# Second mixer of a two-layer encoder trunk: the half swaps before the scans are issued from ScalarE's queue instead of SyncE's

## The chip, the cores and the metric

The kernel runs on one core of a Trainium2 chip. The metric is the device time of one execution in microseconds (us); the median over the runs shown is compared. The profile is one further execution, with its own time. TensorE is PE in the profile (its weight load is PEld), VectorE is DVE, ScalarE is ACT, GpSimd is POOL, SyncE is SP. A trailing q (SPq, ACTq) marks the engine's instruction queue, which among other things issues DMAs.

## The reference, cut to what matters

The trunk has two layers on 512 positions of width 1024. Each layer is a mixer, a cross-attention into 256 memory tokens, and a gated convolutional FFN. The change lies in the mixer of the second layer, in its bidirectional S5 state-space half:

```
bu_re = einsum('gph,bsgh->bsgp', bb_re, u);  bu_im = einsum('gph,bsgh->bsgp', bb_im, u)
s = associative_scan(s_t = a * s_(t-1) + bu_t)          # complex, once forward, once backward
y = einsum('ghp,bsgp->bsgh', c_re, s_re) - einsum('ghp,bsgp->bsgh', c_im, s_im)
o_c = gelu(y_f + y_b + d_skip * u) * sigmoid(...)
```

The other half of the mixer is a depthwise convolution of width 31 with a gate and a layer norm. Both halves are projected out together.

## The kernel before

The 512 channels of the S5 part are four blocks (i = 0 to 3), each with two directions (d = 0 forward, 1 backward). Real parts of the states lie on partitions 0 to 63 of a tile and imaginary parts on 64 to 127. A complex rotation therefore needs the tile once as it is and once with its halves swapped. A swap is two DMAs, from one half of the partitions to the other half of a second tile, 128 KB each.

The work of a block runs through stages with one-letter names. The list `CD` at the top of the kernel gives their order by hand, such as `c0 C0 q0 k1 a1 v1 V1 q0 q0 s0 b1 l1 L1`. The stages that matter here:

- `u`, `v`, `g`: projections of 24 matmuls (lines 206 to 208) of 128x512, with a weight load `wr` of 512 KB from SP (line 147), a high part `wh` cut on ACT (line 201) and a low part `wl` on DVE or POOL (line 202).
- `l`, `L`: SP loads the input matrices `bm` (line 1358) and the rotation tables `cst` (line 1363) of a block.
- `c`, `C`: `c_(i, 0)` and `c_(i, 1)`, the function that the diff touches. 8 matmuls of 64 columns (line 1374) give a tile, ACT copies it to T1 (line 1377), two DMAs write T1s (1378, 1379), DVE multiplies by the tables and adds (1380 to 1382), scans (1384 or 1386) and rotates back (1387, 1388).
- `s`: the second swap, T1s to X2s, from SP (1394, 1395). `x`: the sum with it (1402), on DVE or POOL.
- `m`: SP loads three matrices `cm` (1408). `y`: the output matmuls with them (1416, 1418).
- `q`: two taps of the convolution on DVE (1463). `w`, `Z`: tables `ct` from SP (1476) and the convolution as matmuls (1489). `a`, `b`, `A`, `B`: transposes (1336, 1345) with ACT copies (1337, 1353). `f`: gelu of the block (1431, 1433). `k`: one step of the next stage's keys and values, with its own weight loads.

A planner with its own costs orders the instructions of each engine when the program is built. For most stages `pinned` adds that the first instruction of a stage on PE and the first on SP stay behind those traced before them; a `q` is held so on DVE. ACT isn't held. Every engine and every queue takes its instructions strictly in the planned order, so an SP DMA that waits holds up all later DMAs of SP. A weight load also waits until one of three `wr` buffers is free; `cm` has three buffers and `ct` two.

ACT issues DMAs at only one other place, line 581 in the first mixer.

Of the kernel before, what the change touches and what calls it, by code (L numbers as in the profile page):

```python
# [90 lines left out]
def trunk(ctx, tc, xT, memT, pos, vec, amask, cmask, bmask,  # L91
          w_z, w_ab, w_abv, w_oab, w_xq, w_xk, w_xv, w_xo, w_up, w_dn, wg2,
          w_cd, w_glu, w_ocd, s5v, s5b, s5bs, s5c, s5cs, ctab, out, upto=99):
    nc = tc.nc
# [8 lines left out]
    def nm(p):  # L103
        n_[0] += 1
        return f"{p}_{n_[0]}"
# [32 lines left out]
    def tp_ps():  # L138
        return PS.tile([128, 512], F32, tag="tp", bufs=2, name=nm("tp"))
# [1118 lines left out]
    def mixer_cd(norm, nnext, kv):  # L1258
# [3 lines left out]
        def b2(tag, bufs):  # L1262
            return T.tile([128, S], F32, tag=tag, bufs=bufs, name=nm(tag))
# [101 lines left out]
        def c_(i, d):  # L1365
            BM, cst = tab[i, d], rot[i, d]
            ct, st, rt = cst[:, 0], cst[:, 1], P.tile([128, S], F32, tag="nsq", bufs=2, name=nm("rt"))
            A.activation(g3(rt), rho[:, 32 * d + 8 * i:32 * d + 8 * i + 8].unsqueeze(2).to_broadcast([128, 8, 64]),
                         AF.Copy)
            V.memset(g3(rt)[:, :, 63 * d:63 * d + 1], 0.0)  # L1370
            fl = (lambda v: g3(v)) if d == 0 else (lambda v: g3(v)[:, :, ::-1])
            tp = tp_ps()
            for g in range(8):
                PE.matmul(tp[:, 64 * g:64 * g + 64], BM[:, 128 * g:128 * g + 128], Rg[i][:, 64 * g:64 * g + 64],  # L1374
                          start=True, stop=True)
            t1, t1s = b2("T1", 3), b2("T1s", 2)
            A.activation(t1, tp, AF.Copy)
            nc.sync.dma_start(t1s[0:64], t1[64:128])
            nc.sync.dma_start(t1s[64:128], t1[0:64])
            V.tensor_tensor(g3(t1), g3(t1), fl(ct), ALU.mult)  # L1380
            V.tensor_tensor(g3(t1s), g3(t1s), fl(st), ALU.mult)
            V.tensor_tensor(t1, t1, t1s, ALU.add)
            if d == 0:
                V.tensor_tensor_scan(t1s, rt, t1, 0.0, op0=ALU.mult, op1=ALU.add)
            else:
                V.tensor_tensor_scan(t1s[:, ::-1], rt[:, ::-1], t1[:, ::-1], 0.0, op0=ALU.mult, op1=ALU.add)
            V.tensor_tensor(g3(t1), g3(t1s), fl(ct), ALU.mult)
            V.tensor_tensor(g3(t1s), g3(t1s), fl(st), ALU.mult)
            X[i, d] = t1, t1s
# [139 lines left out]
        def k_(i):  # L1529
            for _ in range(min(i, len(ksteps))):  # L1530
                if ksteps[0] == kv.norm:
# [5 lines left out]
        stage = {"u": (PS_, u_), "a": (PS_, a_), "b": (PS_, b_), "x": ((), x_), "y": (PS_, y_),  # L1537
                 "l": (PS_, l_), "L": (PS_, r_), "m": (PS_, m_), "s": (PS_, s_),
                 "c": (PS_, lambda i: c_(i, 0)), "C": (PS_, lambda i: c_(i, 1)),
                 "f": (PS_, f_), "v": (PS_, lambda i: half0(4 + i)), "V": (PS_, v_),  # L1540
                 "g": (PS_, lambda i: half0(8 + i)), "G": (PS_, g_),
# [192 lines left out]
```

## Time and profile before

| What | Value |
|---|---|
| median of 3 runs | 1631.38 us (1629.17 to 1634.59) |
| profiled execution, its own time | 1632.09 us |
| span of the profiled execution | 1630.3 us |
| busy: PE, DVE, ACT, POOL | 96%, 66%, 43%, 23% of the span |
| mean granted TensorE clock | 0.982 of full speed |
| second mixer's S5 blocks | about 875 to 1050 us in the span |

The span runs from the first to the last instruction; 1.8 us of the execution's own time lie outside it. Busy shares are averages over stages with different limits. In the rows below a bracket is the idle time of the engine just before an instruction and what ended it.

### The profile page before, as it was taken

What the parts mean: (1) busy time and instruction counts of PE and PEld (TensorE: products, weight loads), DVE (VectorE), ACT (ScalarE), POOL (GpSimd) and SP (SyncE); (2) the same over time, 40 slices, a digit from 0 to 9 for tenths busy, and PEclk for the clock granted to TensorE, in tenths of its full rate; (3) what the DMA queues carried; (4) which work ended last, traced back from release to release, by engine and by line L of the source; (5) the groups of instructions that cost most, each with busy time, mean ns of one, the idle gap of its engine ahead of it and who ended that gap; (6) DMA issues with size and microseconds to landing.
All of it is one profiled execution on the core that took longest, in us unless ns stands there. A gap on an engine that the chain in (4) does not pass through costs nothing.

```text
span 1630.3 us, 20958 instructions
## 1 busy us (share of the span) xinstructions
PE 1570.0 (96%) x8036; PEld 1313.0 (81%) x8036; DVE 1079.4 (66%) x1475; ACT 707.4 (43%) x1089; POOL 368.2 (23%) x371
## 2 busy tenths in 40 slices
PE   8999999999999898989999898989999999999997
PEld 6788889888888777877887777878888888888887
DVE  7587766466578789489655997275755766636644
ACT  5464755354453334234335233364543544414423
POOL 8411000000079844445500101230000111100101
PEclk9999999999999999999999899999999999999999
DMA  5323334131222345435444574533312232323231
GB/s 176 109 78 90 120 98 134 51 117 52 78 87 91 105 128 153 145 110 163 145 157 148 181 279 128 186 127 135 108 40 78 92 102 92 102 92 103 83 112 64
DMA packets 76118, 189.11 MB, mean 116 GB/s; under 512 B 8369, under 2 KB 27441, under 8 KB 76017
## 3 DMA queue, kind: packets, MB, share of 16 engines
q1 hardware_dynamic: 75376, 186.58, 35.5%
q8 instruction: 63, 1.03, 0.3%
q0 software_dynamic: 320, 1.05, 0.2%
q14 instruction: 39, 0.31, 0.1%
q10 hardware_dynamic: 320, 0.13, 0.0%
HBM read 162.43 MB, written 19.01 MB: 111 GB/s over the span
## 4 chain that ended last, share of the span: by engine, by line
PE 69%; DVE 13%; POOL 6%; DMA 3%; issue 3%; ACT 3%; SPq 1%; ACTq 0%; DVEq 0%; POOLq 0%
PE mm L208 20%; PE mm L206 19%; PE mm L207 19%; DVE wl L202 2%; PE mm L737 2%; PE sc L1489 1%; DVE t L972 1%; DVE dv L1463 1%; DVE t L971 1%; PE tp L724 1%; PE tp L1374 1%; POOL t L1139 1%; POOL wl L202 1%; DVE tr L1138 1%; PE sc L206 1%
## 5 line engine op out<-in xcount | busy, mean ns | idle before, releaser
L201 ACT ACTIVATE wh<-wr 128x1024 fp32r<-128x1024 f32 (+1 forms) x229 | 239.1, 1044 | 419.7 <-PE mm L207 316.8
L208 PE MATMUL mm<-hg,wl 128*128 128x512 f32 x1000 | 393.7, 394 | 13.8 <-DVE wl L202 13.4
L206 PE MATMUL mm<-hg,wh 128*128 128x512 f32 x1000 | 398.3, 398 | 2.0 <-ACT wh L201 2.0
L207 PE MATMUL mm<-hg,wh 128*128 128x512 f32 x1000 | 392.8, 393 | 0.0
L202 DVE TENSOR_TENSOR wl<-wr,wh 128x1024 fp32r<-128x1024 f32 (+1 forms) x215 | 279.0, 1298 | 68.3 <-ACT wh L201 66.3
L208 PEld LDWEIGHTS mm<-hg,wl 128*128 128x128 f32 x1000 | 189.7, 190 | 57.5 <-DVE wl L202 16.2
L206 PEld LDWEIGHTS mm<-hg,wh 128*128 128x128 f32 x1000 | 190.1, 190 | 44.4 <-ACT wh L201 2.7
L207 PEld LDWEIGHTS mm<-hg,wh 128*128 128x128 f32 x1000 | 189.8, 190 | 40.0 <-issue 1.2
L208 PE MATMUL mm<-g,wl 128*128 128x512 f32 x324 | 126.7, 391 | 2.4 <-DVE wl L202 2.4
L206 PE MATMUL mm<-g,wh 128*128 128x512 f32 x324 | 126.9, 392 | 0.0
L207 PE MATMUL mm<-g,wh 128*128 128x512 f32 x324 | 126.2, 389 | 0.0
L976 POOL TENSOR_TENSOR t<-t,t 128x512 f32<-128x512 f32 x22 | 28.9, 1314 | 422.8 <-ACT t L182 422.8
L968 DVE TENSOR_TENSOR u<-mm,R 128x512 f32<-128x512 f32 x88 | 60.3, 687 | 74.2 <-PE mm L208 74.0
L970 ACT ACTIVATE t<-u,vt 128x512 f32<-128x512 f32 x88 | 70.8, 807 | 50.0 <-DVE u L968 49.8
L986 DVE TENSOR_TENSOR h<-mm,h 128x512 f32<-128x512 f32 x40 | 27.6, 691 | 87.9 <-PE mm L208 87.9
L971 DVE SCALAR_TENSOR_TENSOR t<-u,vt,t 128x511 f32<-128x511 f32 x88 | 77.3, 879 | 8.1 <-ACT t L970 8.1
L972 DVE SCALAR_TENSOR_TENSOR t<-u,vt,t 128x511 f32<-128x511 f32 x88 | 79.2, 901 | 4.1 <-DMA dct<-tr 1.5
L208 PEld LDWEIGHTS mm<-g,wl 128*128 128x128 f32 x324 | 60.8, 188 | 16.1 <-DVE wl L202 3.2
L182 ACT ACTIVATE t<-t 128x512 f32<-128x512 f32 x44 | 27.8, 632 | 103.5 <-DVE t L972 103.4
L207 PEld LDWEIGHTS mm<-g,wh 128*128 128x128 f32 x324 | 60.9, 188 | 12.4
L206 PEld LDWEIGHTS mm<-g,wh 128*128 128x128 f32 x324 | 60.9, 188 | 12.4
L202 POOL TENSOR_TENSOR wl<-wr,wh 128x1024 fp32r<-128x1024 f32 x14 | 35.0, 2503 | 140.7 <-ACT wh L201 121.5
(522 smaller groups left out, 3040.9 us busy)
## 6 DMA issues: line engine op xcount, KB each, us to landing
wr<-in_w_up SPq DMA_DIRECT2D x88, 512.0 KB
wr<-in_w_dn SPq DMA_DIRECT2D x32, 448.0 KB
wr<-in_w_ab SPq DMA_DIRECT2D x16, 512.0 KB
wr<-in_w_xv SPq DMA_DIRECT2D x16, 512.0 KB
wr<-in_w_xk SPq DMA_DIRECT2D x16, 512.0 KB
wr<-in_w_xq SPq DMA_DIRECT2D x16, 512.0 KB
wr<-in_w_xo SPq DMA_DIRECT2D x16, 512.0 KB
wr<-in_w_dn SPq DMA_DIRECT2D x16, 512.0 KB
```

What stands on the lines that cost most here:

```text
L182: tabbed(A.activation(dst, src, fn, **kw))
L201: A.activation(H[:, :n], raw[:, :n], AF.Copy)
L202: (eng or V).tensor_tensor(L[:, :n], raw[:, :n], H[:, :n].bitcast(F32), ALU.subtract)
L206: PE.matmul(ps, lH, rH, start=start, stop=False)
L207: PE.matmul(ps, lH, rL, start=False, stop=False)
L208: PE.matmul(ps, lL, rH, start=False, stop=stop)
L737: PE.matmul(onat[:, 64 * j:64 * j + 64], pt[:, 128 * jt:128 * jt + 128], va[:, jt, 64 * hd:64 * hd + 64], start=jt == 0, stop=jt == 3)
L968: V.tensor_tensor(u, ps, R, ALU.mult)
L970: A.activation(t, u, AF.Identity, scale=vc(f"cw{l}", 44 + i), bias=vc(f"cb{l}", i))
L971: V.scalar_tensor_tensor(t[:, 1:], u[:, :S - 1], vc(f"cw{l}", i), t[:, 1:], op0=ALU.mult, op1=ALU.add)
L972: V.scalar_tensor_tensor(t[:, :S - 1], u[:, 1:], vc(f"cw{l}", 88 + i), t[:, :S - 1], op0=ALU.mult, op1=ALU.add)
L976: (V if l == 0 else G).tensor_tensor(res[1], res[1], res[0], ALU.mult)
```

## The change

The two DMAs that swap the halves of T1 are issued from ScalarE's queue. There they stand on the engine that makes their source, T1. The second swap (`s`) stays on SP, as do all loads.

```
@@ c_(i, d)
             t1, t1s = b2("T1", 3), b2("T1s", 2)
             A.activation(t1, tp, AF.Copy)
-            nc.sync.dma_start(t1s[0:64], t1[64:128])
-            nc.sync.dma_start(t1s[64:128], t1[0:64])
+            nc.scalar.dma_start(t1s[0:64], t1[64:128])
+            nc.scalar.dma_start(t1s[64:128], t1[0:64])
             V.tensor_tensor(g3(t1), g3(t1), fl(ct), ALU.mult)
```

`c_` runs eight times, so 16 DMAs change queues. A stage `c` or `C` then holds no SP instruction that could be pinned.

## Rows read from the trace of the kernel before

**Rows 1.** The page: busy time and share of each engine; chain that ended last.
```profile
PE 1570.0 (96%) x8036; PEld 1313.0 (81%) x8036; DVE 1079.4 (66%) x1475; ACT 707.4 (43%) x1089; POOL 368.2 (23%) x371
...
PE 69%; DVE 13%; POOL 6%; DMA 3%; issue 3%; ACT 3%; SPq 1%; ACTq 0%; DVEq 0%; POOLq 0%
```

**Rows 2.** Windows: stretch, length, busy time by engine, granted clock, DMA share, GB/s.
```profile
940.00:960.00 20.00, 16.63 (x96) 13.34 (x96) 19.93 (x30) 5.40 (x9) 0.00 (x0) 0.93 0.65 234
960.00:980.00 20.00, 20.00 (x115) 17.42 (x114) 16.45 (x25) 10.13 (x17) 2.68 (x1) 0.90 0.89 325
```

**Rows 3.** SP's own waits, 866 to 1030 us: total, times, longest.
```profile
SPq L1378 <- ACT T L1377: 58.3, 6, 19.1
SPq L1394 <- DVE T1s L1388: 34.0, 6, 10.3
```

**Rows 4.** Chain of waits in the second mixer: start, us, what.
```profile
890.85 0.61 ACT T L1377
...
892.06 2.37 DMA T1s<-T
...
918.33 2.37 DMA T1s<-T
...
953.84 5.49 DMA cm<-dc
...
997.78 4.08 DMA T1s<-T
...
1025.34 5.75 DMA wr<-in_w_xv
```

**Rows 5.** Lines 1378, 1379 and 581: ns min/median/max of one DMA issue.
```profile
L1378 SPq DMA_DIRECT2D T1s<-T x8: 461/467/549, 891.5 to 997.3; - x8
L1379 SPq DMA_DIRECT2D T1s<-T x8: 582/588/590, 892.1 to 997.8; - x8
L581 ACTq DMA_DIRECT2D d_rt<-rt x4: 342/444/448, 68.1 to 69.4; - x4
```

**Rows 6.** SP's timeline: start, length, line, DMA, count.
```profile
908.08 0.48 SPq L147 DMA_DIRECT2D wr<-in_w_xv  x1
...
918.97 0.58 SPq L1408 DMA_DIRECT2D cm<-dmt  x1
...
937.10 0.45 SPq L147 DMA_DIRECT2D wr<-in_w_cd  x1
...
953.35 0.87 SPq L1408 DMA_DIRECT2D cm<-dc  x2
...
998.46 1.68 SPq L1476 DMA_DIRECT2D ct<-in_ctab  x2
1000.24 0.86 SPq L147 DMA_DIRECT2D wr<-in_w_xv  x2
```

**Rows 7.** ACT's timeline behind the second copy of block 0.
```profile
893.12 0.58 ACT L1337 ACTIVATE at<-tp 64x512 f32<-64x512 f32 x1
```

**Rows 8.** PE's timeline: first output matmul of block 1 (y1).
```profile
956.80 0.91 PE L1416 MATMUL sc<-cm,Rg 128*64 128x128 f32 x4 [2.10 <-DMA cm<-dmt]
```

**Rows 9.** Windows around the output matmuls of block 1, then block 2 (columns as rows 2).
```profile
956.80:966.20 9.40, 8.83 (x49) 7.88 (x50) 8.66 (x14) 2.71 (x5) 0.00 (x0) 0.64 0.80 300
996.50:1002.00 5.50, 5.50 (x50) 5.29 (x49) 2.05 (x4) 1.19 (x2) 0.00 (x0) 1.00 0.85 215
```

**Rows 10.** DVE's timeline, 920 to 1002 us.
```profile
920.78 0.69 DVE L1380 TENSOR_TENSOR T<-T,cst 128x512 f32<-128x512 f32 x1 [0.78 <-DMA T1s<-T]
...
963.61 1.23 DVE L202 TENSOR_TENSOR wl<-wr,wh 128x1024 fp32r<-128x1024 f32 x1
...
969.83 0.42 DVE L245 SCALAR_TENSOR_TENSOR macc<-tp,macc 128x256 f32<-128x256 f32 x1 [0.71 <-ACT macc L244]
...
973.45 0.69 DVE L1327 TENSOR_TENSOR uT<-mm,R 128x512 f32<-128x512 f32 x1 [0.50 <-PE mm L208]
...
1001.94 0.69 DVE L1380 TENSOR_TENSOR T<-T,cst 128x512 f32<-128x512 f32 x1 [1.39 <-DMA T1s<-T]
```

## The prediction

> **What bounds the kernel now.** I read the page first. PE is busy for 96% of the span and carries 69% of the chain that ended last, and the queues of SP and ACT carry about 1% of it together [rows 1]. A DMA issue alone is therefore worth almost nothing over the whole kernel. What counts is whether something in the second mixer stands behind an issue. The windows came next. From 940 to 960 DVE is busy for 19.93 of 20 us and PE for only 16.63, so here DVE sets the pace and PE waits. From 960 to 980 PE is full again, at a granted clock of 0.90, and the DMAs move 325 GB/s [rows 2]. Then I asked what SP waits for. For 58.3 us, in six waits of up to 19.1 us, it stands at line 1378 until ACT has written T1. That wait is what the change takes off SP. A second of its kind, 34.0 us at the swaps behind the scans, stays [rows 3]. Last I followed the chain of waits through the blocks, to see which of the things queued on SP behind the first wait end late enough to matter.
>
> **The swap itself.** The chain shows ACT's copy of block 0 starting at 890.85 and lasting 0.61 us. The DMA's own part starts at 892.06, at the start of the second issue, and takes 2.37 us to the first DVE multiply; the same 2.37 us stands at 918.33 for block 1 [rows 4]. Between them lies SP's first issue, 0.47 us in the median; the second takes 0.59 [rows 5]. The copy ends at 891.46 and the second issue starts at 892.06, so 0.60 us passes in which the first issue takes most: SP starts as good as at once, and no handshake of size is there to be saved. ACT's own DMA issues exist in this trace, at line 581: 0.44 us in the median, for a smaller transfer of another shape [rows 5]. Bounds for the two issues together are thus 0.88 us (twice that row) and 1.06 us (SP's rows). A gain of 0.2 us per swap is the most, over the three or so swaps on the chain 0.6 us. I take SP's values, as the transfer is the same one, and so a gain of 0.
>
> **What ACT pays.** Sixteen issues of about 0.53 us are 8.4 us more on ACT's queue. The cover is ACT's idle time: it is busy for 5.40 us of 20 and 10.13 of 20 in the two windows [rows 2]. Behind a swap stand the next copy of T1, the `wh` cut of a projection, and copies of transposes. The one place that is tight is block 0: right behind the copy for the backward direction ACT starts a transposes' copy of 0.58 us at 893.12, and a second such one follows in the code [rows 7]. If these two go ahead of the second swap, that swap is up to 1.2 us late and DVE with it; if the swap goes first, the copies are late and PE has 24 matmuls in front of the work that needs them. The code has the swap first, so I take 0 and keep the 1.2 us for the range.
>
> **What SP gains, and where it ends.** The loads queued behind the eight swaps leave earlier. Three groups count.
>
> *Block 1's `cm`.* After its weight load at 937.10 SP issues nothing until the swaps of block 2, and two of the three `cm` loads follow behind these at 953.35 [rows 6]. Their buffers were block 0's, whose output matmuls stand well ahead in `CD`, so I see only the wait for T1 between. The chain runs through this transfer, 5.49 us of it [rows 4]. PE waits 2.10 us for it [rows 8] and then needs 9.40 us at a granted clock of 0.64, where block 2's same work takes 5.50 us at clock 1.00 [rows 9]. So 2.10 + (9.40 - 5.50) = 6.0 us is what PE would gain if `cm` lay ready. I don't book it in full, because DVE stands behind it. The next projection needs `wl`, which DVE makes at 963.61 in an unbroken row of work [rows 10]; an earlier PE waits there. DVE itself waits for the PE and ACT work that would come earlier only 0.71 us at 969.83 and 0.50 us at 973.45 [rows 10]. DVE's order kept, 1.2 us passes on.
>
> *Block 1's own swaps.* The `cm` and weight loads that now leave at 918.97 [rows 6] are block 0's, find their buffers unused, and can leave behind the weight load at 908.08 [rows 6], about ten microseconds earlier. So they are in flight when block 1's swaps go. DVE waits for the second of these, 0.78 us [rows 10], and is nearly full afterwards, so a later landing is a loss of the same size. From below, the landing stays at 2.37 us, which is what it takes with the `cm` issue right behind it; the nearest row with a costly neighbour is the 4.08 us at 997.78, with `ct` right behind at 998.46 [rows 4, 6], 1.71 more. The upper end is a landing like that of a load on a busy queue, 5.75 us [rows 4], 3.4 more. Of the two near rows one says 0 and one 1.7; I take the middle, a loss of 0.9 us.
>
> *Block 3's swaps.* The `ct` and weight loads of 998.46 and 1000.24 move ahead of the swaps that they now follow [rows 6]. DVE waits 1.39 us for the second swap [rows 10]. If those loads are done by then, 4.08 becomes 2.37 and 1.7 us is won; if they are in full flow, 4.08 becomes 5.75 and 1.7 us is lost. They would leave when the convolution's matmuls have freed the `ct` buffers, which is shortly before the swaps and so between the two; I take 0.
>
> The row at 997.78 says that transfers of one queue already slow one another here. The Trainium skill, page "DMA: Bandwidth & Descriptors", section "Issuing engines are not separate DMA queues", speaks against the change: DMAs issued by different engines run on the same 16 DMA engines, and a second issuer saves only issue time on the sequencer. By that rule alone the sum would be 0 for the swaps and their 8.4 us on SP would fall into its waits; the row agrees in so far as a load beside a swap costs the swap time.
>
> **Sum.** 0 for the issue, 0 on ACT, 1.2 gained at block 1's outputs, 0.9 lost at its swaps, 0 at block 3: 0.3 us gained. The profiled execution took 1632.09 us (span 1630.3 and 1.8 around it), so 1631.8 by its time. It lies 0.7 above the median of the runs, 1631.38; in their terms the forecast is 1631.1. Its own range is from 1.2 + 1.7 + 0.6 = 3.5 gained to 1.2 - 3.4 - 1.7 - 1.2 = 5.1 lost with all bounds at once; 1628 to 1635 is what I give it.
>
> **Rivals.** *The gain at `cm` passes on.* The planner orders DVE and ACT anew, and with SP free it may set `wl` and the scans of block 2 earlier. Then all 6.0 us reach the end: 1625.4, or 1623.7 with block 3's 1.7 as well. For it speaks that PE has this time to give [rows 8, 9]; against it that DVE is full for 20 us [rows 2] and none of its work is removed.
>
> *The swaps collide with the released loads.* This one ends slower. On a queue of their own the swaps share the DMA engines with everything that SP no longer holds back. If each lands like the loads beside it, in 5.75 us, block 1 loses 3.4, block 2 as much (at most, since the chain doesn't run through its swaps) and block 3 1.7, together 8.5 less the 1.2 gained: 1638.7. It decides where 4.9 us are lost net, from an extra of 2.6 us per swap on (2.6 + 2.6 + 0.9 - 1.2), a landing of 5.0 us. For it speak the DMA share of 0.89 in the window from 960 and 0.80 to 0.85 beside the outputs [rows 2, 9]; against it that the swap at 918.33 landed in 2.37 us with three loads issued behind it.
>
> *Nothing moves.* The swaps behind the scans hold SP too, 34.0 us [rows 3], and the loads may be held by them, by buffers, or by the planned order, and leave when they leave now. Then it is 1631.4.
>
> **Numbers.** Forecast 0.45, nothing moves 0.17, gain passes on 0.19, collision 0.13; 0.06 is for a reordering with effects elsewhere, shared between both signs. A measurement of this kernel can tell about 0.3% from no change, 4.9 us. That gives faster 0.22, same 0.61, slower 0.17. The range runs from 1626 to 1637 and leaves out the outer parts of both rivals.
>
> **What would show it.** The T1s DMAs on ACT's queue, 0.03 us or so behind the copy, with landings between 2.4 and 4.1 us; SP's wait at line 1378 gone, its time now at 1394; `cm` of block 1 issued near 938, no wait before line 1416, and block 1's outputs in about 5.5 us at full clock; and then PE waiting for `wl` or DVE near 962. The forecast fails if DVE's order around 953 to 975 changes, if swaps land later than 5 us, or if ACT sets a `wh` cut of 1 us between T1 and its swap on the chain.

## The result, and the profile after

The change makes the kernel slower. Its median is 1642.65 us (10 runs, 1639.88 to 1654.63) beside 1634.15 us for the kernel before (10 runs, 1629.17 to 1637.11), a ratio of 1.0066 with a 95% interval of 1.0047 to 1.0085. The medians are 8.5 us apart, and 0.66% of 1634.15 is 10.8 us. The forecast was 1631.1 us with a range from 1626 to 1637. The profiled execution took 1640.68 us with a span of 1638.9; the kernel before took 1632.09 with 1630.3. So 8.6 us are to be found.

The page of the changed kernel shows next to nothing of it. Busy times stand as they stood, and the chain's shares within three points [rows 1]. ScalarE's queue, q10, has 1600 packets where it had 320.

```profile
PE 1570.4 (96%) x8036; PEld 1311.1 (80%) x8036; DVE 1077.7 (66%) x1475; ACT 707.9 (43%) x1089; POOL 367.2 (22%) x371
...
q1 hardware_dynamic: 74096, 184.48, 34.8%
q10 hardware_dynamic: 1600, 2.23, 0.6%
...
PE 72%; DVE 12%; POOL 6%; issue 3%; DMA 3%; ACT 3%; SPq 1%; ACTq 0%; DVEq 0%; POOLq 0%
```

The windows, with the columns of [rows 2], show where it happens. From 920 to 940 the DMAs are nearly idle and DVE is less busy than it was (19.18 us before); from 940 to 960 PE works 12.57 of 20 us, where it worked 16.63, and its granted clock is 0.74 in place of 0.93 [rows 2].

```profile
920.00:940.00 20.00, 20.00 (x124) 16.70 (x122) 16.89 (x23) 4.60 (x9) 2.65 (x1) 1.00 0.12 31
940.00:960.00 20.00, 12.57 (x61) 9.82 (x60) 18.60 (x25) 5.40 (x7) 1.26 (x1) 0.74 0.92 336
960.00:980.00 20.00, 20.00 (x128) 16.46 (x128) 15.63 (x28) 9.65 (x18) 0.00 (x0) 1.00 0.41 119
```

To size a loss one needs marks that every kernel has. I take the start of ACT's copy of T1 (line 1377) in the forward direction of each block. Before, it starts at 890.85, 913.78, 949.63 and 994.86 us for blocks 0 to 3; after, at 891.70, 914.41, 958.78 and 1003.76. From block 0 to block 1 nothing is lost (22.93 and 22.71). From block 1 to block 2 it is 35.85 before and 44.37 after, so **8.5 us are lost there**. From block 2 to block 3 it is 45.23 and 44.98. One stretch carries everything. ACT's timeline before:

```profile
913.78 0.60 ACT L1377 ACTIVATE T<-tp 128x512 f32<-128x512 f32 x1 [2.68 <-PE tp L1374]
...
949.63 1.16 ACT L1377 ACTIVATE T<-tp 128x512 f32<-128x512 f32 x2
```

And after:

```profile
958.78 0.60 ACT L1377 ACTIVATE T<-tp 128x512 f32<-128x512 f32 x1 [0.37 <-PE tp L1374]
```

DVE's timeline in that stretch, two lines of the kernel before and then the changed kernel:

```profile
917.50 0.69 DVE L1380 TENSOR_TENSOR T<-T,cst 128x512 f32<-128x512 f32 x1 [1.15 <-DMA T1s<-T]
...
925.45 0.67 DVE L1327 TENSOR_TENSOR uT<-mm,R 128x512 f32<-128x512 f32 x1
```

```profile
920.06 1.23 DVE L202 TENSOR_TENSOR wl<-wr,wh 128x1024 fp32r<-128x1024 f32 x1 [2.91 <-ACT wh L201]
924.33 0.69 DVE L1327 TENSOR_TENSOR uT<-mm,R 128x512 f32<-128x512 f32 x1 [3.05 <-PE mm L208]
924.94 0.74 DVE L1463 SCALAR_TENSOR_TENSOR dv<-dv,vt,dv 128x509 f32<-128x509 f32 x1
925.60 2.84 DVE L1380 TENSOR_TENSOR T<-T,cst 128x512 f32<-128x512 f32 x1
```

The order is new. Before, DVE took the first multiply of block 1 (L1380) at 917.50, then `wl`, the second multiply at 920.78 [rows 10], the scans, and block 2's projection sum (L1327) only at 925.45. After, the planner has `wl`, the sum and a tap ahead of the first multiply. DVE stands 2.91 us for `wh` and 3.05 us for block 2's matmuls, and the multiply starts at 925.60 with no bracket: it waits for its place and for no transfer. Its 2.84 us in place of 0.69 stand beside a `wl` of GpSimd's at 925.24; before, a tap at 927.92 took 2.85 beside the same `wl` at 927.88, so this is no part of the loss.

The chain that ended last says how this reaches PE (start, us, what):

```profile
910.73 7.06 PE tp L1374 x32
...
924.94 0.74 DVE dv L1463
925.68 2.75 DVE T L1380
...
932.77 1.13 DVE T1s L1384
...
939.95 1.19 DVE T1s L1388 x2
...
941.84 0.47 SPq L1394
...
943.63 4.23 DMA wr<-in_w_xv
947.90 0.04 issue
947.95 1.07 ACT wh L201
949.01 0.04 issue
949.05 0.80 PE mm L206
```

The multiplies are 8 us late, and with them the scans and the rotation back (L1388). SP issues the second swap at 941.84 where it did at 932.67. Behind it on SP stands a weight load, which lands 4.23 us after its issue, then `wh` is cut, and only then PE has work. PE's timeline gives the larger part of the price, to which the lower clock of that window adds; before, it shows no wait between 926 and 952 us:

```profile
947.76 0.80 PE L206 MATMUL mm<-hg,wh 128*128 128x512 f32 x1 [7.35 <-ACT wh L201]
```

SP's timeline shows the loads. `cm` of block 0 leaves at 909.30, ten microseconds before its 918.97 in [rows 6], `cm` of block 1 at 946.61 in place of 952.72. SP's wait for T1 of [rows 3] is gone; SP now waits at line 1394, for the first swap's landing (46.2 us) and for the scans (45.8; before, 34.0).

```profile
909.30 0.46 SPq L1408 DMA_DIRECT2D cm<-dmt  x1
...
940.57 0.47 SPq L1394 DMA_DIRECT2D X2s<-T1s  x1
...
943.63 0.45 SPq L147 DMA_DIRECT2D wr<-in_w_xv  x1
...
946.61 0.39 SPq L1408 DMA_DIRECT2D cm<-dmt  x1
```

SP's waits, in total, times and longest:

```profile
SPq L1394 <- DMA T1s<-T: 46.2, 4, 15.2
SPq L1394 <- DVE T1s L1388: 45.8, 5, 18.1
```

ACT's timeline: the swap is issued 0.03 us behind its copy (914.41 + 0.60 = 915.01), and the second issue of the backward swap runs beside the `wh` cut, at 918.98.

```profile
914.41 0.60 ACT L1377 ACTIVATE T<-tp 128x512 f32<-128x512 f32 x1 [2.53 <-PE tp L1374]
915.04 0.47 ACTq L1378 DMA_DIRECT2D T1s<-T  x1
915.55 0.61 ACTq L1379 DMA_DIRECT2D T1s<-T  x1
...
918.97 1.06 ACT L201 ACTIVATE wh<-wr 128x1024 fp32r<-128x1024 f32 x1 [0.55 <-ACT T L1377]
918.98 0.59 ACTq L1379 DMA_DIRECT2D T1s<-T  x1
```

Last, the queues of the changed kernel: packets, MB and share of the 16 engines' time, from 917 to 919 us and then from 919 to 921.

```profile
q1 hardware_dynamic: 219, 0.79, 100.9%
q10 hardware_dynamic: 1, 0.00, 0.3%
...
q1 hardware_dynamic: 129, 0.46, 69.5%
q10 hardware_dynamic: 125, 0.22, 36.1%
```

The forward swap was issued by 916.2. In the first of these windows SP's queue fills the engines with its released loads and ScalarE's moves one packet.

Two causes are thus in sight. **Order:** VectorE's planned order in block 1 puts block 2's sum ahead of the multiplies. **Landing:** the released loads hold up the swaps, and the order only fills the time until they land. They are the theory and its rival in what follows.

### The profile page after: what moved, and what is told of

Its sections match the earlier page's. It is cut to its first block, busy times and chain, and to the rows that moved or that the text cites. A ratio compares the mean times of both kernels' runs of the same rounds, so it can differ in the third digit from the quotient of the medians.

```text
span 1638.9 us, 20960 instructions
## 1 busy us (share of the span) xinstructions
PE 1570.4 (96%) x8036; PEld 1311.1 (80%) x8036; DVE 1077.7 (66%) x1475; ACT 707.9 (43%) x1089; POOL 367.2 (22%) x371
## 4 chain that ended last, share of the span: by engine, by line
PE 72%; DVE 12%; POOL 6%; issue 3%; DMA 3%; ACT 3%; SPq 1%; ACTq 0%; DVEq 0%; POOLq 0%
PE mm L208 20%; PE mm L207 20%; PE mm L206 20%; DVE wl L202 2%; PE mm L737 2%; PE sc L1489 1%; DVE t L972 1%; PE tp L1374 1%; DMA wr<-in_w_xv 1%; DVE t L971 1%; PE tp L724 1%; DVE t L976 1%; POOL wl L202 1%; POOL t L1139 1%; PE sc L208 1%
```

## The experiments

Each kernel was timed beside the kernel before on the same chip; a ratio is against that kernel, with its 95% interval. Profiles are of one execution, so their spans differ by several microseconds for reasons elsewhere (in its profile the kernel of e8 reaches block 0 some 14 us late, and by its median it is not slower). Stretches between the marks are freer of this. Two profiles of the changed kernel give 112.06 and 112.14 us from block 0's mark to block 3's, and the kernel before and e4 give 104.01 and 103.87. The columns `b1 to b2` and `b0 to b3` are such stretches in us.

| Kernel | Swaps on ScalarE | Ratio to before | b1 to b2 | b0 to b3 |
|---|---|---|---|---|
| before | none | | 35.85 | 104.01 |
| changed | all | 1.0066 [1.0047, 1.0085] | 44.37 | 112.06 |
| e1 sum put back | all | 1.0029 [1.0005, 1.0054] | 37.20 | 105.92 |
| e2 | block 1 | 1.0067 [1.0041, 1.0094] | 44.35 | 113.72 |
| e3 | 0, 2, 3 | 1.0008 [0.9981, 1.0035] | 35.81 | 103.04 |
| e4 | block 0 | 1.0005 [0.9983, 1.0026] | 35.88 | 103.87 |
| e5 late order alone | none | 1.0045 [1.0021, 1.0068] | 43.62 | 111.21 |
| e6 sum put back | block 1 | 0.9999 [0.9975, 1.0023] | 37.38 | 103.24 |
| e7 as e6, loads held | block 1 | 1.0022 [0.9996, 1.0048] | 37.74 | 104.80 |
| e8 loads early | none | 1.0001 [0.9975, 1.0027] | 34.44 | 101.62 |
| e9 `cm` of block 1 early | none | 0.9976 [0.9958, 0.9993] | 35.81 | 100.94 |
| e10 as e9, `bm` too | none | 0.9987 [0.9969, 1.0004] | 36.95 | 99.80 |
| e11 weights freed | all | 1.0049 [1.0029, 1.0069] | 34.76 | 110.26 |
| e12 changed again | all | 1.0058 [1.0036, 1.0081] | 44.25 | 112.14 |

### Which block, and the sum put back (e1 to e4)

In e1 one ordering edge is added to the changed kernel: the sum of a block's projection (L1327) stays behind the backward scan (L1386) of the block before. It waits for nothing on the chip; it only binds the planner. In e2 to e4 the engine of the first swaps is chosen by block. The code is shortened here and below: `NoSync` stands for the kind of edge, and the lines that fill `scans` and `muls` are left out.

```
 # e1, in u_(i), beside the change
-            V.tensor_tensor(uT[i], ps, R, ALU.mult)
+            us_ = V.tensor_tensor(uT[i], ps, R, ALU.mult)
+            scans.get(i - 1) and tc.add_manual_dep(us_.ins, scans[i - 1], NoSync)
 # e2 (i == 1), e3 (i != 1), e4 (i == 0), in c_(i, d)
-            nc.scalar.dma_start(t1s[0:64], t1[64:128])
-            nc.scalar.dma_start(t1s[64:128], t1[0:64])
+            (nc.scalar if i == 1 else nc.sync).dma_start(t1s[0:64], t1[64:128])
+            (nc.scalar if i == 1 else nc.sync).dma_start(t1s[64:128], t1[0:64])
```

> All swaps on ACT as in the changed kernel; one ordering edge keeps block 2's first sum (line 1327) behind block 1's scans on DVE, which restores DVE's order of before around block 1. Theory 'planned order' (the loss is that DVE does the next block's sum, and waits for it, ahead of block 1's multiplies): 5 to 8 us come back, 0 to 4 us above the kernel before, and DVE starts block 1's first multiply at about 918. Theory 'late landing' (the swaps wait behind the loads that SP now issues early, whatever DVE does): 0 to 3 us come back, 5 to 9 above before, and DVE waits at line 1380 of block 1 until 921 to 923.

> Only block 1's four swap DMAs on ACT, those of blocks 0, 2 and 3 on SP as before. If block 1 carries the loss (both theories say so, as the first difference of the two traces lies between 918 and 941 us): 6 to 9 us above the kernel before. If the loss is spread over the blocks, as the collision rival of the prediction had it: 2 to 4 us.

> Block 1's swaps on SP as before, those of blocks 0, 2 and 3 on ACT. If block 1 carries the loss: -2 to +3 us against the kernel before (the late landing of block 3 costs up to 2, the earlier cm of block 1 may give some back). If spread: 4 to 6 us above.

> Only block 0's swaps on ACT; SP's queue is empty there and DVE and PE keep the order of before. All theories: within 1.5 us of the kernel before, and 2.4 us from the second issue to the first multiply. If issuing from ACT costs something by itself (a slower issue, copies held up behind it): 1 us or more above, with the multiply later.

Measured: block 1 alone (e2) carries the whole loss, with 44.35 us from block 1 to block 2 like the changed kernel, and the same order on DVE. With all blocks but block 1 (e3) the kernel's time can't be told from before, nor with block 0 alone (e4). The issue from ScalarE thus costs nothing by itself that these runs show. With the sum put back behind the scans (e1) the stretch falls from 44.37 to 37.20; 1.4 us of loss remain in it and 1.9 us up to block 3. The first multiply is still late, and now for the transfer. DVE's timeline of e1, block 1, whose copy of T1 starts at 915.11:

```profile
923.33 0.69 DVE L1380 TENSOR_TENSOR T<-T,cst 128x512 f32<-128x512 f32 x1 [1.35 <-DMA T1s<-T]
```

By itself e1 doesn't decide between the two. Its time, 4.7 us above the kernel before [0.8 to 8.8], lies between the two ranges that were expected, and its first multiply starts where the landing theory put it. By the stretch the order carries most of the loss in block 1; the late landing is real, and it may have a share. e1's ratio of 1.0029 is still above one, and neither block 1 alone in this order (e6, below) nor the others alone (e3) show that rest. By the profiles it stands behind block 2's mark: from block 0's mark to block 2's e1 takes 60.12 us and e6 60.10, from there to block 3's 45.80 and 43.14. The edge puts back the sum and not the whole order. Between the first multiplies of block 1 and block 2 DVE has 26 taps in e1, 20 in e6 and 23 in the kernel before. Whether that is the rest isn't tested.

### The order alone, with every swap on SP (e5)

The reverse of e1: the kernel before, in which only block 1's multiplies are bound behind block 2's sum. SP and PE take the same instructions in the same order as before. DVE and ACT are ordered anew behind the multiplies, so the run measures the late multiplies together with what the planner makes of them.

```
-            V.tensor_tensor(uT[i], ps, R, ALU.mult)
+            us_ = V.tensor_tensor(uT[i], ps, R, ALU.mult)
+            i == 2 and [tc.add_manual_dep(x.ins, us_.ins.name, NoSync) for x in muls[1]]
...
+            # muls[i]: the instructions of lines 1380 and 1381
```

> Every swap is on SP, as before the change, and no load moves. Only VectorE's order in block 1 is made that of the changed kernel: the first multiplies of block 1's rotation (L1380, L1381) are put behind block 2's projection sum (L1327), with the weight's low part (L202) ahead of it. If the planned order carries the larger part of the loss, block 1's first multiply moves from 917.50 us to about 924.5 (the sum ends when TensorE's matmuls are done, 924.33 in the changed kernel less 0.6), and the kernel is 5 to 7 us slower than before. If the late landing of the swaps carries the loss and the order only fills the time until then, the swap lands at 917.5 as before, other work is merely drawn ahead of it, and the kernel is within 2 us of before.

Measured: 1.0045 [1.0021, 1.0068], 7.3 us of 1632.91 (the medians are 6.2 apart), and 43.62 us from block 1 to block 2 where the changed kernel has 44.37. No DMA changed its queue and no load was released. DVE's timeline of e5:

```profile
930.37 0.69 DVE L1327 TENSOR_TENSOR uT<-mm,R 128x512 f32<-128x512 f32 x1 [5.15 <-PE mm L208]
930.98 0.68 DVE L1380 TENSOR_TENSOR T<-T,cst 128x512 f32<-128x512 f32 x1
```

PE's timeline of e5, some 20 us later:

```profile
951.37 0.79 PE L206 MATMUL mm<-hg,wh 128*128 128x512 f32 x1 [4.77 <-ACT wh L201]
```

A weight's high part ends PE's wait. It is the same picture without the change: the sum waits for PE, the multiply follows without a wait of its own, and PE stands for a weight that SP issued at 947.33, behind the second swaps of 945.47. The order alone is enough for 7.8 of the 8.5 us in this stretch, and by the ratios for 7.3 of 10.8 us, with intervals that overlap. This settles which of the two carries the larger part: the order.

### What the landing is worth (e6 to e8)

In e6 only block 1's swaps are on ScalarE and the sum is put back by e1's edge, so that the landing beside released loads is what is left. In e7 SP also stores 2 KB of the second T1, and so waits for it again ahead of its loads. In e8 all swaps are on SP and `m0` stands ahead of `c1` in `CD` (with e1's edge), so that the loads of block 0's `cm` leave early on the swaps' own queue.

```
 # e7, behind the swap of (i, d) == (1, 1)
+            nc.sync.dma_start(d_hold[1][d], t1[64:65])
 # e8, in CD
-q0 q0 c1 C1 m0 k1 q0 u2
+q0 q0 m0 c1 C1 k1 q0 u2
```

> Only block 1's swaps are on ScalarE; block 2's projection sum is kept behind block 1's scans, as in the kernel before; SP's loads are released early. What is left is the landing of block 1's swaps beside SP's loads. If these hold the swaps up, the first multiply starts 5 to 8 us after the copy that makes the source, where it took 3.1 us before, and the kernel is 2 to 5 us slower than before. If only the order cost time, the kernel is within 1.5 us of before.

> As the run with only block 1's swaps on ScalarE and the order kept, with one thing more: SP stores 2 KB of block 1's second T1 to a scratch, so that its later loads wait for this T1 as they did before the change. If the released loads are what delays the swaps, these land as before (first multiply about 3 us after the copy of T1), and the kernel is within 1.5 us of before. If ScalarE's queue is slow in itself, the first multiply stays 5 to 8 us behind and the loss of 2 to 5 us stays too.

> All swaps are on SP. The three loads of block 0's output tables (L1408) are put ahead of block 1's swaps in SP's order, so that they leave some ten us earlier, as they did in the changed kernel; block 2's projection sum stays behind block 1's scans. If loads in flight delay a swap whichever queue it is on, the first multiply of block 1 starts 5 to 8 us after the copy of T1 and the kernel is 2 to 5 us slower. If only a second queue is held up by a full first one, the swap lands in about 2.4 to 3 us and the kernel is within 1.5 us of before.

The second issue of block 1's forward swap in ACT's timeline of e6, and the first multiply in DVE's:

```profile
915.26 0.60 ACTq L1379 DMA_DIRECT2D T1s<-T  x1
...
922.52 0.69 DVE L1380 TENSOR_TENSOR T<-T,cst 128x512 f32<-128x512 f32 x1 [1.57 <-DMA T1s<-T]
```

The first multiplies of e7, forward and backward:

```profile
919.40 0.69 DVE L1380 TENSOR_TENSOR T<-T,cst 128x512 f32<-128x512 f32 x1 [1.13 <-DMA T1s<-T]
...
925.01 0.69 DVE L1380 TENSOR_TENSOR T<-T,cst 128x512 f32<-128x512 f32 x1 [1.90 <-DMA T1s<-T]
```

Issue and multiply of e8, forward, the issue from SP:

```profile
928.58 0.60 SPq L1379 DMA_DIRECT2D T1s<-T  x1
...
934.13 0.69 DVE L1380 TENSOR_TENSOR T<-T,cst 128x512 f32<-128x512 f32 x1 [0.47 <-DMA T1s<-T]
```

A landing is counted from the start of the second issue to the multiply. In the kernel before it is 2.58 us (914.92 to 917.50). In e6 it is 7.26 (915.26 to 922.52). With the loads held, in e7, the first swap takes 2.59 (916.81 to 919.40): with SP's loads held back ScalarE's queue is as quick as SP's. The second swap of e7 was issued at 920.21, just behind the held loads, which left from 919.97, and takes 4.80. In e8 the swap stands behind early loads on SP's own queue and takes 5.55 (928.58 to 934.13). So **loads in flight delay the swap on either queue**. A second queue isn't needed for it; what the change did was to let the loads go first. Whether the second queue adds to it (7.26 beside 5.55) one profile of each can't tell. In e6 one load more stands ahead of the swap, the weight load of 512 KB issued at 910.59, which e8 has behind its swaps; at the 0.79 MB that q1 moved in 2 us of the changed kernel it would take some 1.3 us, an estimate, and that is most of the difference.

The time is another matter. e6 loses 4.7 us at the landing, 1.5 us at block 2's mark, and nothing by block 3; its ratio is 0.9999. My expectation of 2 to 5 us isn't borne out, though e6's interval reaches from 4.1 us faster to 3.8 slower: behind the multiplies there is slack for a swap that is 5 us late, and in the changed kernel and e5 there isn't for multiplies that are 7 to 8. e8, at 1.0001, shows no loss either. e7 repaired the first landing, but its time, 1.0022 [0.9996, 1.0048], decides nothing.

### The gain that was booked (e9, e10)

All swaps are on SP, with e1's edge. In e9 `m1` moves from behind `C2` to behind `L2`, so that only block 1's `cm` leaves ahead of block 2's swaps. In e10 `l1` is put ahead of `v1` as well, and block 1's `bm` ahead of block 0's second swaps.

```
-b2 l2 L2 q1 q0 g2 q0 G2 q1 c2 C2 m1 A2 k1
+b2 l2 L2 m1 q1 q0 g2 q0 G2 q1 c2 C2 A2 k1
 # e10 as well
-v1 V1 q0 q0 s0 b1 l1 L1 k1 g1
+l1 v1 V1 q0 q0 s0 b1 L1 k1 g1
```

> All swaps are on SP and block 2's sum stays behind block 1's scans. Only the three loads of block 1's output tables (L1408) move ahead of block 2's swaps in SP's order. This is the one gain that the prediction booked, by itself. If the earlier TensorE work passes on only as far as VectorE waits for it, no wait is left before L1416 and the kernel is 0 to 2.5 us faster than before, which is too little to be told. If it passes on in full, it is 5 to 6 us faster.

> As the run with block 1's output tables early, and block 1's input tables (L1358) also ahead of block 0's swaps behind the scans, so that TensorE doesn't wait for them near 910 us, where it waited 4.36 us before. If block 1 sets the pace from that wait on, its copy of T1 comes 3 to 4 us earlier and the kernel is 3 to 6 us faster than before; if VectorE's work behind block 0 sets it, T1 comes earlier and block 2's T1 doesn't, and the kernel is within 2 us of before.

Measured: e9 is faster than both kernels, 0.9976 [0.9958, 0.9993], 3.9 us of 1630.1. It lies between the two expectations, and the interval, 1.1 to 6.9 us, reaches into both. `cm` leaves at 939.02, PE has no wait ahead of its output matmuls, and the window of SP's loads and PE's work reads:

```profile
940.00:960.00 20.00, 20.00 (x128) 16.50 (x127) 19.89 (x29) 7.13 (x11) 0.00 (x0) 1.00 0.82 292
```

PE is busy for all 20 us where it had 16.63, at a granted clock of 1.00 where it had 0.93 [rows 2], and DVE is as full as it was. Part of it is paid back further on: PE waits 0.69 us for `wh` at 974.39 and 2.04 us for GpSimd's `wl` at 977.16, where the kernel before has no such waits. From block 0 to block 3 e9 gains 3.1 us. From 952 us on the planner also orders PE, DVE and ACT anew, so the 3.9 us are the early `cm` and what the planner made of it. In e10, counted from block 0's mark, block 1's copy of T1 comes 5.8 us earlier than before and block 2's 4.7; up to block 3 it gains 4.2 us. Its ratio, 0.9987 [0.9969, 1.0004], is not better than e9's and not clear of the time before, though e9's edit is in it. So the size of e9's gain is uncertain, and whether the early `bm` is worth anything isn't decided.

### Does the loss sit in the weights behind SP's second swaps? (e11, e12)

If PE's 7.35 us come only from a weight load held behind the late second swaps, freeing that load should end the loss, late order or not. In e11 block 1's second swaps are on ScalarE too; e12 is the changed kernel again.

```
-                nc.sync.dma_start(xs[0:64], t1s[64:128])
-                nc.sync.dma_start(xs[64:128], t1s[0:64])
+                (nc.scalar if i == 1 else nc.sync).dma_start(xs[0:64], t1s[64:128])
+                (nc.scalar if i == 1 else nc.sync).dma_start(xs[64:128], t1s[0:64])
```

> The changed kernel, and block 1's swaps behind the scans (L1394, L1395) issued by ScalarE too, so that the weight loads behind them on SP don't wait for the late scans. VectorE still puts block 2's sum ahead of block 1's multiplies. If the late order costs time because TensorE then stands 7.35 us for weights that SP held behind those swaps, that wait is gone, the weights are issued near 911 us in place of 943, and the kernel is within 3 us of the kernel before. If VectorE's lateness reaches TensorE by its results, the wait only changes its name, and the kernel stays 6 to 11 us slower than before.

> The changed kernel once more, beside the run in which the weights are freed, so that the two stand against the same runs of before. Every theory has it 0.5 to 0.9% slower than before, with TensorE standing about 7 us for a weight's high part near 948 us.

Measured: 1.0049 [1.0029, 1.0069] beside 1.0058 [1.0036, 1.0081]. The two can't be told apart. The weight left at 928.30, some ten us later than expected when counted from block 0's mark, and the wait near 948 is gone (34.76 us from block 1 to block 2, even less than before), yet from block 2 to block 3 it takes 52.62 us where it took 45.23. PE's timeline of e11, a block later:

```profile
989.18 1.22 PE L206 MATMUL mm<-wh,mg 128*128 128x512 f32 x2 [8.32 <-ACT wh L201]
```

Before it, block 2's first multiply in DVE's timeline and the DMAs in SP's:

```profile
970.43 0.69 DVE L1380 TENSOR_TENSOR T<-T,cst 128x512 f32<-128x512 f32 x1
...
983.14 0.53 SPq L1394 DMA_DIRECT2D X2s<-T1s  x1
...
984.37 0.58 SPq L147 DMA_DIRECT2D wr<-in_w_xv  x1
```

e11's profile reaches block 0's mark 6.8 us later than the changed kernel's, so times are counted from that mark. Block 2's T1 is copied after 57.6 us (58.8 before the change), but DVE comes to its multiply only after 71.9 us and without a wait (63.1 before). Block 2's second swaps therefore go out after 84.6 us, as late as in the changed kernel (84.5; before, 74.6), hold the next weight load, and PE stands 8.32 us there. The wait at the weight is the place where the loss is paid; its cause is DVE's lateness, and that passes on to the next such place. Some of that lateness is again planned order, as DVE has two taps and a `wl` more ahead of this multiply than before.

## Why the prediction was wrong, point by point

**The swap's issue, 0: right as far as the runs can tell.** ScalarE issues in 0.47 us (468 ns in the median) 0.03 us behind its copy. Block 0 goes from the copy to the first multiply in 3.64 us after (891.70 to 895.34) and in 3.70 before (890.85 to 894.55), and e4 is at 1.0005 [0.9983, 1.0026].

**What ScalarE pays, 0: right.** The `wh` cut that the planner put between the two halves of block 1's backward swap runs beside the second issue, and e6, which has the same cut there, is at 0.9999.

**Block 1's `cm`, a gain of 1.2: the mechanism right, the size probably too small.** The 2.10 us of waiting ahead of L1416 [rows 8] are gone in the changed kernel. Alone, in e9, the early `cm` is worth 3.9 us [1.1 to 6.9 by the interval], between the 1.2 booked, which the interval just includes, and the 6.0 that PE had to give. "DVE's order kept, 1.2 us passes on" counted only the two waits of DVE in [rows 10]; PE's later wait for `wl`, which the forecast named, came at 977 us and for GpSimd's. The reading that DVE sets the pace from 940 to 960 us doesn't hold by the waits: before, PE's waits there are 2.10 and 0.47 us for `cm` and 0.70 for DVE. In the changed kernel the gain is nowhere to be seen: from block 2 to block 3 it takes 44.98 us, 0.25 less than before.

**Block 1's own swaps, a loss of 0.9: both halves wrong.** The landing was forecast at 2.37 us with 5.75 as the upper end; it measured 7.26 in e6. The row that I trusted, 2.37 us with `cm` issued right behind, had its loads behind the swap on the same queue; the case to come had them ahead, and e8 shows 5.55 for that on one queue. The price, "a loss of the same size", failed in the other direction: 4.7 us of late landing cost nothing that e6's time shows (0.9975 to 1.0023).

**Block 3's swaps, 0: right in the sum, with a landing off.** The chain of the changed kernel has 5.96 us at the T1s DMA of 1004.90, above the 5.75 given as the upper end; e3, which holds this swap and has it land 6.4 us after its second issue (995.93 to 1002.34), is at 1.0008 [0.9981, 1.0035].

**The step that failed** is the assumption under all of these, "DVE's order kept". The text named a reordering twice, at `cm` as a hope (the gain passes on) and in the chances with 0.06, and looked for it around 953 to 975. It came at 917 to 940, in block 1, and is worth by itself 7.3 us (e5: 1.0045) where the whole change costs 10.8 (1.0066); in the stretch from block 1 to block 2 it is 7.8 of 8.5 us. The terms of the sum that were worked out are all small, and e6 and e3, at 0.9999 and 1.0008, can't be told from their 0.3 us. The collision rival came nearest in its number, 1638.7, and landings did exceed its 5.0 us, but it is not the larger cause: in e6 and e8 a landing is late and the time is that of before. With all blocks' swaps on ScalarE, in e1, 4.7 us remain with the sum put back, and late landings may have a share in these.

**What stays open.** Why the planner puts block 2's sum ahead isn't shown. It does so when block 1's swaps stand on ScalarE and no edge forbids it (e2, e11, e12), and not when only the other blocks' do (e3). Nor is it settled what e1's remaining 0.3% [0.05%, 0.54%] is.

Of the issuing engine, the Trainium skill, page "DMA: Bandwidth & Descriptors", section "Issuing engines are not separate DMA queues", states that a second issuer saves only the sequencer's time, since the transfers run on the same 16 engines. e3, e4 and e6 agree in so far as none of them is clear of the time before: 1.0008, 1.0005 and 0.9999.

## What to carry to other kernels

When a planner orders the engines, moving a DMA to another issuer is also a change of order on engines that the diff doesn't touch: compare the orders of both kernels before pricing the transfer, and bind what must not move with an ordering edge (e6 and e8 carry one, at 0.9999 and 1.0001). A released queue doesn't only start its loads earlier; it puts them ahead of the small transfer that was moved, and that transfer then lands with them. If a load is what one wants earlier, move the load: e9 moved three and gained 3.9 us [1.1 to 6.9], where moving the swaps away from them lost 10.8 (0.66% of 1634.15).

## What the runs showed of the hardware

ScalarE's queue didn't share the DMA engines evenly with SP's. From 917 to 919 us, with the forward swap issued by 916.2, q1 moved 219 packets at a share of 100.9% and q10 moved one. q10 rose to 125 packets only as q1 fell to 69.5%. The next two blocks look alike in the changed kernel: q10 has one packet from 960 to 962 us and 245 in the 2 us behind, and from 1006 to 1008 us it is at 4.5%, then at 79.0%. What holds the second queue back, the engines or the making of its descriptors, no run here shows. The Trainium skill, page "DMA: Bandwidth & Descriptors", section "Queues, rings and completion order", states that an engine takes turns between the queues that have work, a whole packet of one queue at a time, typically some 9 to 17 descriptors. The rows above don't settle whether that holds here. If the profile's packets are those of the page, one to 219 is not turn by turn; if each of them is a descriptor, 219 are about 14 to each of the 16 engines, which is one turn.
